# GpSimd operations that wait for the all-SBUF VectorE operation ahead of them in the plan

## The chip, the cores and the metric

The kernel runs on one core of a Trainium2 chip. The metric is device time in microseconds (us). The kernel before takes 2153.72 us, the median of 3 runs (2153.02 to 2155.7). A core has four engines that compute here: TensorE (PE, with its weight loads shown as PEld), VectorE (DVE), ScalarE (ACT) and GpSimd (POOL). SyncE (SP) issues the DMAs. Each engine works through its instructions in the order in which they stand in the program, and waits on semaphores where it needs what another engine makes. PE reads its operands from SBUF and adds into PSUM; DVE and ACT reach both; POOL works on SBUF alone.

## The reference

One decoder layer on x of 1 x 1024 x 1024 (sequence 1024, width 1024), in float32:

```python
h = rmsnorm(x, norm_mix)
proj = h @ w_in                       # z, xBC, dt, lru_y, lru_x, q, k, v, g, three gates
y_ssd, y_lru, y_ret = ssd_mixer(...), rglru_mixer(...), retention_mixer(...)
branch_d = jnp.einsum('bskw,kwd->bskd', branches, w_branch)
merged = jnp.sum(sigmoid(gate_pre) * branch_d, axis=2)
x = x + merged @ w_o
h = rmsnorm(x, norm_ffn)
a, u = jnp.split(h @ ffn_w_in, 2, axis=-1)          # 3072 columns each
a = causal_dwconv(a, ffn_conv_w, ffn_conv_b)        # 3 taps
x = x + (gelu(a) * u) @ ffn_w_out
return rmsnorm(x, norm_final)
```

Most of the work is dense products: the input projection, three branch products, `w_o`, and the two products of the FFN.

## The kernel before

**Products.** Activations lie transposed, 128 channels x 1024 positions, in two halves of 512 positions. Every dense product is made in "quads": a 2 x 2 block product (two output strips, two halves of positions) by a Strassen-Winograd scheme of seven products instead of eight. Each float32 operand is split into a high part (ACT copies it into the matmul's type, `h`) and a low part (the rest, `l`), and a product is three matmuls: high x high, high x low, low x high (L450, L451, L452). A quad sums in the PSUM banks x, y and z, and what leaves a bank is copied or added by ACT (L260) and DVE (L475, L480) into SBUF buffers named `e_...`.

**Sets and strips.** The activations of a stage are a set of seven operands B11, B21, T1, T2, T3, B22, T4, four tiles each, made by `build_set`: `sub` subtracts two SBUF tiles into PSUM (L342, and L353 for the second difference, tiles `hT`, `y2T`, `g0T` ...), and `split` makes `h` on ACT and `l` on DVE or POOL (L336, `g0B22l` and the like). The sets follow one another: h (the projection), y0, y2 and y1 (the branches), mg (`w_o`), h2 (FFN in), g0, g1 and g2 (FFN out, a third of the inner channels each). The weights of each quad come by DMA in strips (`wr_...`); `Quad.operand` makes their sums S1 to S4 (L407), S1 and S3 in PSUM banks of their own, and `Quad.prep` splits them (ACT, and L420 on DVE or POOL: `fo00A12l` is quad fo00's low part of A12). When a quad's result is complete, its `use` function runs: L1162 and L1166 gate and add the branches (`e_br`), L1230 multiplies the FFN's two halves (`cv_fa`), L1253 adds the residual (`e_fo`). The FFN's convolution (`conv`) pads a tile with three zeros (MEMSET, L522, `o_fa`), scales it on ACT and adds two taps on DVE (L528).

**What sets the order.** All operations are recorded first, with their buffers, the engines that may do them and a due time. `Plan.schedule` then plays the program through with an estimated duration for each, gives each operation an engine and a start, and the program is issued in the order of the starts, under `manual_schedule`, so that each engine's order is the plan's. The variable `port` of the planner keeps two kinds of operation from overlapping in the plan: any POOL operation, and a DVE operation with the mark `lock`, which is set where nothing that the operation reads lies in PSUM:

```python
o.lock = "DVE" in engs and len({id(b) for b in r if b.tag in PSUMS}) == 0
...
ok = not (port > t and (e == "POOL" or (e == "DVE" and o.lock))) and fits(o)
...
if e == "POOL" or (e == "DVE" and o.lock):
    port = t + dur
```

This holds in the plan, with its estimated durations. On the chip the engines run by their semaphores alone, and in the kernel before nothing orders a POOL operation against a DVE operation that shares no data with it.

Of the kernel before, what the change touches and what calls it, by code (L numbers as in the profile page):

```python
# [240 lines left out]
class K:  # L241
# [1103 lines left out]
    def run(self, gl):  # L1345
        tc, nc = self.tc, self.nc
        with tc.tile_pool(name="small", bufs=1) as small, \
                tc.tile_pool(name="big", bufs=1) as pool, \
                tc.tile_pool(name="psum", bufs=1, space=PSUM) as psum, \
                tc.tile_pool(name="dram", bufs=1, space=DRAM) as dpool:  # L1350
            self.small, self.dpool = small, dpool
            self.load_consts()
            self.record(gl)
            slots = dict(SLOTS)
            for key in self.OPS:
                for p in range(4):
                    for s in "hl":
                        slots[f"{key}{s}{p}"] = 1
            ops = self.pl.schedule(slots)
            eng = {"PE": nc.tensor, "ACT": nc.scalar, "DVE": nc.vector, "POOL": nc.gpsimd, "DMA": nc.sync}  # L1360
            with tc.manual_schedule():
                for op in ops:
                    for b in op.alloc:
                        pl = psum if b.tag in PSUMS else pool
                        b.t = pl.tile(b.shape, b.dt, name=b.name, tag=f"{b.tag}_{b.slot}")
                    op.fn(eng[op.eng])


def pairs():
# [97 lines left out]
```

## Time and profile before

| | |
|---|---|
| median of 3 runs | 2153.72 us |
| the profiled execution | 2152.18 us, of which 2150.3 are the span of its instructions |
| mean granted PE clock | 0.987 |
| ACT busy | 1265.2 us (59%) |
| HBM read and written | 236.34 MB, 94.37 MB |
| POOL's operations | 399 |

The profile is of one execution. Its page gives the busy time of each engine, and views of the trace give single instructions: the start in us from the start of the span, the duration, the engine, the line of the kernel, the operation, the tile written and the tiles read, and in square brackets how long the engine had been idle and which instruction released it. A row with "x3" stands for three such instructions in a row, with their time together. Stage windows cut the span in pieces and give each engine's busy time in each. A row that begins with an engine and has "<-" and another engine is a group of waits: the time in total, how many, and the longest.

### The profile page before, as it was taken

What the parts mean: (1) busy time and instruction counts of PE and PEld (TensorE: products, weight loads), DVE (VectorE), ACT (ScalarE), POOL (GpSimd) and SP (SyncE); (2) the same over time, 40 slices, a digit from 0 to 9 for tenths busy, and PEclk for the clock granted to TensorE, in tenths of its full rate; (3) what the DMA queues carried; (4) which work ended last, traced back from release to release, by engine and by line L of the source; (5) the groups of instructions that cost most, each with busy time, mean ns of one, the idle gap of its engine ahead of it and who ended that gap; (6) DMA issues with size and microseconds to landing.
All of it is one profiled execution on the core that took longest, in us unless ns stands there. A gap on an engine that the chain in (4) does not pass through costs nothing. (4 is left out here: it accounts for less than half of the span.)

```text
span 2150.3 us, 27983 instructions
## 1 busy us (share of the span) xinstructions
PE 2076.7 (97%) x9394; PEld 1661.1 (77%) x9394; DVE 1585.5 (74%) x2469; ACT 1265.2 (59%) x2182; POOL 490.6 (23%) x399
## 2 busy tenths in 40 slices
PE   8999999999999999999999999989999999999997
PEld 4788887778888887777777777768888888877775
DVE  7878889976544456665789889796676666787786
ACT  6656665455766689998744445465444444645453
POOL 3000023431011111111253332331111111233332
PEclk9999999999999999999999999989999999999999
DMA  5333335544344444446578755713322222366764
GB/s 179 118 106 125 108 122 168 167 141 139 130 145 155 150 156 152 150 157 207 188 236 280 245 181 191 240 57 105 103 103 80 78 89 79 108 226 224 227 212 159
DMA packets 148176, 332.56 MB, mean 155 GB/s; under 512 B 16448, under 2 KB 17216, under 8 KB 148032
## 3 DMA queue, kind: packets, MB, share of 16 engines
q1 hardware_dynamic: 148032, 330.78, 46.6%
q8 instruction: 73, 1.20, 0.2%
q14 instruction: 71, 0.58, 0.1%
HBM read 236.34 MB, written 94.37 MB: 154 GB/s over the span
## 5 line engine op out<-in xcount | busy, mean ns | idle before, releaser
L260 ACT ACT_TABLE_LOAD x94 | 120.6, 1283 | 1.8 <-DVE acc_fin L585 0.2
L260 ACT ACTIVATE cv_fa<-cv_fa 128x512 f32<-128x512 f32 x48 | 30.4, 632 | 56.4 <-DVE cv_fa L528 56.4
L528 DVE SCALAR_TENSOR_TENSOR cv_fa<-o_fa,consts,cv_fa 128x512 f32<-128x512 f32 x48 | 56.7, 1182 | 0.9
L1230 POOL TENSOR_TENSOR cv_fa<-cv_fa,o_fu 128x512 f32<-128x512 f32 x21 | 32.6, 1551 | 99.8 <-ACT o_fu L260 99.8
L528 DVE SCALAR_TENSOR_TENSOR cv_fa<-e_ff,consts,cv_fa 128x512 f32<-128x512 f32 x48 | 38.0, 792 | 4.9 <-ACT cv_fa L260 4.9
L260 ACT ACTIVATE mt<-ps_a,acs 128x128 f32<-128x128 f32 x128 | 38.9, 364 | 0.3
L1253 POOL TENSOR_TENSOR e_fo<-e_fo,xl 128x512 f32<-128x512 f32 x13 | 16.8, 1294 | 75.4 <-DVE e_fo L480 66.7
L260 ACT ACTIVATE e<-ps_a 64x512 f32<-64x512 f32 x32 | 19.0, 593 | 13.7 <-PE ps_a L855 13.2
L944 PE MATMUL ps_l<-lxh,lwh 128*128 128x512 f32 x64 | 26.0, 406 | 0.3
L1052 PE MATMUL ps_ry<-sc,vt 128*128 128x128 f32 x128 | 23.8, 278 | 2.2 <-DVE rst L1040 1.6
L1162 DVE TENSOR_TENSOR e_br<-e_br,gl 128x512 f32<-128x512 f32 x19 | 23.5, 1237 | 3.0 <-DMA gl<-gt 2.5
L867 DVE TENSOR_TENSOR mt<-mt,cbt 128x512 f32<-128x512 f32 x22 | 16.8, 763 | 11.8 <-ACT mt L260 11.7
L946 PE MATMUL ps_l<-lxh,lwl 128*128 128x512 f32 x64 | 25.2, 394 | 0.0
L945 PE MATMUL ps_l<-lxl,lwh 128*128 128x512 f32 x64 | 25.2, 394 | 0.0
L965 DVE TENSOR_TENSOR li<-li,lx 128x512 f32<-128x512 f32 x16 | 11.1, 693 | 18.4 <-ACT li L260 18.4
L1230 DVE TENSOR_TENSOR cv_fa<-cv_fa,e_ff 128x512 f32<-128x512 f32 x23 | 22.6, 984 | 2.3 <-ACT cv_fa L260 0.3
L1040 DVE SCALAR_TENSOR_TENSOR rst<-rst,ps_kv 128x128 f32<-128x128 f32 x40 | 11.0, 286 | 17.8 <-ACT rst L260 16.1
L475 DVE TENSOR_TENSOR e_ff<-e_ff,z_ff 128x512 f32<-128x512 f32 x24 | 16.5, 687 | 10.0 <-PE z_ff L452 10.0
L965 POOL TENSOR_TENSOR li<-li,lt 128x512 f32<-128x512 f32 x4 | 5.2, 1302 | 78.7 <-ACT lt L260 78.7
L867 POOL TENSOR_TENSOR mt<-mt,cbt 128x512 f32<-128x512 f32 x10 | 13.9, 1394 | 40.3 <-ACT mt L260 38.5
L965 DVE TENSOR_TENSOR li<-li,lt 128x512 f32<-128x512 f32 x12 | 8.3, 693 | 19.8 <-ACT lt L260 19.8
L528 DVE SCALAR_TENSOR_TENSOR cv_xs<-o_xs,consts,cv_xs 128x512 f32<-128x512 f32 x24 | 21.9, 912 | 0.5
(6169 smaller groups left out, 8082.1 us busy)
## 6 DMA issues: line engine op xcount, KB each, us to landing
wr_ff<-in_ffn_in_dram SPq DMA_DIRECT2D x50, 512.0 KB, 3.8
wr_fo<-in_ffn_out_dram SPq DMA_DIRECT2D x43, 512.0 KB, 4.6
wr_br<-in_w_branch_dram SPq DMA_DIRECT2D x36, 512.0 KB, 4.6
yl<-yd SPq DMA_DIRECT2D x60, 256.0 KB, 4.8
gl<-g SPq DMA_DIRECT2D x60, 256.0 KB, 4.5
wr_gt<-in_w_quads_dram SPq DMA_DIRECT2D x24, 512.0 KB, 5.0
gl<-gt SPq DMA_DIRECT2D x48, 256.0 KB, 4.0
g<-cv_fa SPq DMA_DIRECT2D x48, 256.0 KB, 2.1
```

Source lines behind the costliest of these rows:

```text
L260: e.activation(out(), in_(), func, **kw)
L475: k.vec(lambda e, e2=e2, ps=ps: e.tensor_tensor(e2.t[:, O:], e2.t[:, O:], ps.t, ALU.add), [e2, ps], [e2], prio=end)
L528: self.vec(lambda e, s=s: e.scalar_tensor_tensor(cv.t[:, O:], raw.t[:, O - s : W - s], w(taps - 1 - s), cv.t[:, O:], ALU.mult, ALU.add), [ ...
L867: self.vec(lambda e, mt=mt: e.tensor_tensor(mt.t[:, O:], mt.t[:, O:], cbt.t[:, O:], ALU.mult), [mt, cbt], [mt], pool=True)
L944: e.matmul(p_.t, wh.t[:, s], h.t, start=(k == 0), stop=False)
L945: e.matmul(p_.t, wh.t[:, s], l.t, start=False, stop=False)
L946: e.matmul(p_.t, wl.t[:, s], h.t, start=False, stop=(k == 1))
L965: mul = lambda a, b_: self.vec(lambda e: e.tensor_tensor(a.t[:, o], a.t[:, o], b_.t[:, o], ALU.mult), [a, b_], [a], pool=True)
L1052: e.matmul(py.t[:, d], at(x, s), at(sc, s), start=True, stop=first)
L1162: self.vec(lambda e: e.tensor_tensor(out.t[:, o], ap(), g.t[:, o], ALU.mult), [buf, g], [out], pool=not ps)
L1230: self.vec(lambda e: e.tensor_tensor(a.t[:, o], a.t[:, o], u.t[:, o], ALU.mult), [a, u], [a], pool=True)
L1253: self.vec(lambda e: e.tensor_tensor(out.t[:, o], ap(), x.t[:, o], ALU.add), [buf, x], [out], pool=not ps)
```

## The change

After each operation of the plan is issued, the kernel notes the last DVE operation that has `lock` (nothing that it reads lies in PSUM; where it writes does not matter) and whose function returns its instruction. Every POOL operation that follows in the plan gets a dependency on it. Nothing else is added.

```diff
@@ -1358,12 +1358,20 @@
             ops = self.pl.schedule(slots)
             eng = {"PE": nc.tensor, "ACT": nc.scalar, "DVE": nc.vector, "POOL": nc.gpsimd, "DMA": nc.sync}
+
+            info = mybir.DependencyInfo(mybir.DependencyClass.Sync, mybir.DependencyReason.DATA)
+            holder = None
             with tc.manual_schedule():
                 for op in ops:
                     for b in op.alloc:
                         pl = psum if b.tag in PSUMS else pool
                         b.t = pl.tile(b.shape, b.dt, name=b.name, tag=f"{b.tag}_{b.slot}")
-                    op.fn(eng[op.eng])
+                    ins = op.fn(eng[op.eng])
+                    if op.eng == "DVE" and op.lock and ins is not None:
+                        holder = ins
+                    elif op.eng == "POOL" and holder is not None:
+                        tc.add_manual_dep(ins.ins, holder.ins.name, info, reason="port order")
+
```

The sums of products in PSUM (S1 and S3, the differences of `sub`, the copies of banks) are already so in the kernel before; the diff does not touch them. The lines behind L1358 move by 8.

In the built program the order of every engine is what it was. The rows of PE and ACT are the same to the last wait. On POOL 145 of 404 rows have other waits, and the rows that wait for DVE go from 185 to 293; on DVE three rows have other waits; on SP 33 rows lose a wait for DVE. The places that the text below speaks of are these. The rows are those of the difference on POOL, with the waits at the end; a row that waits for DVE waits for one particular instruction of it, which the row does not name, and where two rows follow each other without a wait the second is held by the first.

POOL at the start of the branch product with set y2 (`y2B22l` are low parts of that set, made from the loaded tiles `yl`; `br22A11l` is a low part of a weight strip; L1162 gates a result):

```order
+L420 TENSOR_TENSOR br22A11l<-wr_br_10566,br22A11h 128x512 [waits DVE_49,DMAHW3_49,PE_49,Activation_49]
 L1162 TENSOR_TENSOR e_br_10611<-e_br_10611,gl_71_10598 128x512 [waits DVE_49]
 L336 TENSOR_TENSOR y2B22l_10739<-yl_41_10192,y2B22h_10718 128x512 [waits DMAHW6_49,Activation_49]
-L336 TENSOR_TENSOR y2B22l_10787<-yl_51_10246,y2B22h_10725 128x512 [waits Activation_49]
+L336 TENSOR_TENSOR y2B22l_10787<-yl_51_10246,y2B22h_10725 128x512 [waits DVE_49]
 L336 TENSOR_TENSOR y2B22l_10805<-yl_61_10268,y2B22h_10730 128x512 [waits DMAHW5_49,Activation_49]
```

`br22A11l` had no wait for DVE before; it now waits for the second of a pair of differences `y2T` (L342). The second `y2B22l` now waits for the split `br23A11l` (L420).

POOL at the passage from the FFN's first product to its second, where set g0 is made:

```order
-L336 TENSOR_TENSOR g0B11l_16886<-gl_20_13802,g0B11h_16859 128x512 [waits Activation_49]
+L336 TENSOR_TENSOR g0B11l_16886<-gl_20_13802,g0B11h_16859 128x512 [waits DVE_49]
 L336 TENSOR_TENSOR g0B11l_16905<-gl_30_13957,g0B11h_16877 128x512 [waits PE_49,Activation_49]
 L420 TENSOR_TENSOR fo01A12l<-wr_fo_16804,fo01A12h 128x512 [waits DVE_49,DMAHW2_49,PE_49,Activation_49]
-L336 TENSOR_TENSOR g0B22l_17029<-gl_41_14591,g0B22h_17007 128x512 [waits Activation_49]
+L336 TENSOR_TENSOR g0B22l_17029<-gl_41_14591,g0B22h_17007 128x512 [waits DVE_49,Activation_49]
 L420 TENSOR_TENSOR fo02A11l<-wr_fo_16889,fo02A11h 128x512 [waits DVE_49,DMAHW5_49,PE_49,Activation_49]
-L336 TENSOR_TENSOR g0T2l_17096<-gl_20_13802,g0T2h_17054 128x512 [waits Activation_49]
+L336 TENSOR_TENSOR g0T2l_17096<-gl_20_13802,g0T2h_17054 128x512 [waits DVE_49]
 L336 TENSOR_TENSOR g0B22l_17108<-gl_51_14603,g0B22h_17012 128x512
-L336 TENSOR_TENSOR g0B22l_17125<-gl_61_16973,g0B22h_17020 128x512 [waits DMAHW0_49]
+L336 TENSOR_TENSOR g0B22l_17125<-gl_61_16973,g0B22h_17020 128x512 [waits DMAHW0_49,DVE_49]
```

The first `g0B11l` now waits for the split `ff23A22l` (L420) of DVE, the first `g0B22l` for a `g0T` (L342), `g0T2l` for a product `cv_fa` (L1230), and behind `g0T2l` stand three `g0B22l` (the third follows the last row here), the second of them with a wait of its own for the next `g0T`. DVE's rows at that place are the same before and after:

```order
L336 TENSOR_TENSOR g0T1l_17045<-g0T_2_17022,g0T1h_17036 128x512
L528 SCALAR_TENSOR_TENSOR cv_fa_17049<-e_ff_16934,consts,cv_fa_17049 128x512
L407 TENSOR_TENSOR fo00S_2_17066<-wr_fo_17015 128x512
L528 SCALAR_TENSOR_TENSOR cv_fa_17049<-e_ff_16934,consts,cv_fa_17049 128x512
L1230 TENSOR_TENSOR cv_fa_16985<-cv_fa_16985,o_fu_17061 128x512
L420 TENSOR_TENSOR fo02A12l<-wr_fo_16889,fo02A12h 128x512
L1230 TENSOR_TENSOR cv_fa_17049<-cv_fa_17049,e_ff_16907 128x512
L420 TENSOR_TENSOR fo00S1l<-fo00S_2_17066,fo00S1h 128x512
L407 TENSOR_TENSOR fo00S_2_17066<-fo00S_2_17066,wr_fo_16943 128x512
```

The row for which `g0T2l` waits is the second L1230 here; fo00S and the `cv_fa` of L528 stand ahead of it.

POOL where set g1 is made:

```order
 L336 TENSOR_TENSOR g1T2l_17828<-gl_20_17273,g1T2h_17820 128x512 [waits DVE_49,Activation_49]
-L336 TENSOR_TENSOR g1B22l_17862<-gl_41_17365,g1B22h_17802 128x512 [waits PE_49]
+L336 TENSOR_TENSOR g1B22l_17862<-gl_41_17365,g1B22h_17802 128x512 [waits DVE_49,PE_49]
 L420 TENSOR_TENSOR fo12A12l<-wr_fo_17694,fo12A12h 128x512 [waits DMAHW6_49,PE_49,Activation_49]
-L336 TENSOR_TENSOR g1B22l_17927<-gl_61_17765,g1B22h_17822 128x512 [waits DMAHW1_49]
+L336 TENSOR_TENSOR g1B22l_17927<-gl_61_17765,g1B22h_17822 128x512 [waits DMAHW1_49,DVE_49]
 L336 TENSOR_TENSOR g1B22l_17945<-gl_71_17797,g1B22h_17836 128x512 [waits DMAHW5_49]
```

The first `g1B22l` now waits for a `g1T` (L342) besides PE, and the second in this piece for a later split of DVE.

At the start of the kernel the second `hB22l` waits for the second `hT`, and in set h2 the first `h2T2l` for the second of the `h2T` pair that stood beside it.

## The prediction

> **What bounds the kernel now.** I read the engines' shares first, then the span cut by stage, then who TensorE (PE) waits for.
>
> ```profile
> PE 2076.7 (97%) x9394; PEld 1661.1 (77%) x9394; DVE 1585.5 (74%) x2469; ACT 1265.2 (59%) x2182; POOL 490.6 (23%) x399
> ...
> 300.00:780.00 480.00, 471.20 (x2561) 386.71 (x2561) 324.80 (x563) 294.00 (x550) 107.48 (x81) 1.00 0.46 149
> 1000.00:1450.00 450.00, 418.99 (x1738) 332.00 (x1737) 371.09 (x536) 233.06 (x416) 154.22 (x112) 0.97 0.61 202
> 1450.00:1885.00 435.00, 434.95 (x1875) 351.42 (x1873) 295.87 (x438) 220.23 (x374) 69.99 (x70) 1.00 0.27 92
> 1885.00:2150.30 265.30, 241.26 (x1022) 193.30 (x1022) 206.11 (x294) 120.20 (x214) 82.20 (x59) 0.96 0.64 212
> ```
>
> A stage row gives start and end in us, the length, then busy time of PE, PEld, VectorE (DVE), ScalarE (ACT) and GpSimd (POOL), granted clock, DMA share and GB/s. PE is idle 73.6 us (2150.3 - 2076.7), and in bunches: 8.8 in 300 to 780, 31.0 in the branch products up to the FFN's start, 24.0 in the last stage. In 1450 to 1885 it is 0.05: nothing that DVE or POOL save there is worth anything. That stage also gives PE's pace, 435 / 1875 = 0.232 us a matmul.
>
> ```profile
> PE x_fo L450 <- ACT e_fo L260: 8.1, 3, 3.7
> PE x_wo L450 <- ACT e_wo L260: 4.0, 1, 4.0
> PE ss_fin L565 <- DVE acc_fin L585: 3.0, 1, 3.0
> PE y_gt L450 <- DVE e_gt L480: 2.4, 1, 2.4
> PE z_wo L450 <- DVE e_wo L480: 2.3, 1, 2.3
> ```
>
> These are some of PE's longest waits (total, times, longest). The largest names ACT, so the question is what ACT was late for. I follow it at 1888.63.
>
> ```profile
> 1888.63 0.79 PE L450 MATMUL x_fo<-g0B21h,fo00A12h 128*128 128x512 f32 x1 [3.68 <-ACT e_fo L260]
> ...
> 1893.91 0.61 PE L450 MATMUL x_fo<-g0B11h,fo01A11h 128*128 128x512 f32 x1
> ...
> 1886.97 0.63 ACT L260 ACTIVATE cv_fa<-cv_fa 128x512 f32<-128x512 f32 x1 [2.83 <-DVE cv_fa L528]
> ...
> 1863.94 2.39 DVE L336 TENSOR_TENSOR g0B11l<-gl,g0B11h 128x512 fp32r<-128x512 f32 x2
> 1866.26 1.78 DVE L420 TENSOR_TENSOR ff23A22l<-wr_ff,ff23A22h 128x512 fp32r<-128x512 f32 x1
> ...
> 1882.82 0.74 DVE L528 SCALAR_TENSOR_TENSOR cv_fa<-e_ff,consts,cv_fa 128x512 f32<-128x512 f32 x1
> 1883.48 1.79 DVE L407 TENSOR_TENSOR fo00S<-wr_fo 128x512 f32<-128x512 f32 x1
> 1885.19 1.75 DVE L528 SCALAR_TENSOR_TENSOR cv_fa<-e_ff,consts,cv_fa 128x512 f32<-128x512 f32 x1
> ...
> 1890.22 0.68 DVE L1230 TENSOR_TENSOR cv_fa<-cv_fa,e_ff 128x512 f32<-128x512 f32 x1
> ...
> 1883.22 1.50 POOL L336 TENSOR_TENSOR g0T2l<-gl,g0T2h 128x512 fp32r<-128x512 f32 x1 [0.93 <-ACT g0T2h L260]
> 1884.68 5.07 POOL L336 TENSOR_TENSOR g0B22l<-gl,g0B22h 128x512 fp32r<-128x512 f32 x3
> ```
>
> The same SCALAR_TENSOR_TENSOR takes 0.74 us at 1882.82 and 1.75 at 1885.19, where POOL has been at work since 1884.68; a clean TENSOR_TENSOR takes 0.68 (1890.22), one beside POOL 1.78. So an all-SBUF DVE operation that meets a running POOL operation pays 1.0 to 1.1 us, and POOL pays too (5.07 / 3 = 1.69). Through this ACT's cv_fa starts 2.83 late, the copy e_fo queued behind it on ACT is late, and PE stands 3.68. The stall has a second price: the twelve matmuls from 1888.63 to 1893.91 take 5.28 us instead of 12 x 0.232 = 2.8, so 2.5 more.
>
> [...]
>
> **The change part by part.** No instruction is added to or moved on any engine or on the DMA queue; POOL rows gain waits for DVE, and some rows of the DMA queue lose one, which releases nothing earlier, since POOL's wait stands ahead of it. The gain is what is no longer blocked, the cost what becomes late.
>
> *g0, 1888.63.* In the built program g0T2l waits for cv_fa<-cv_fa,e_ff (1890.22), and three g0B22l stand behind it on POOL. None of them is there when DVE runs fo00S and cv_fa: 1.1 + 1.0 = 2.1 earlier on ACT's chain. g0B11l of POOL is held in the same way until ff23A22l (1866.26), which frees that row and the second of the pair ahead of it (2.39 - 2 x 0.68), 1.1 + 1.0 = 2.1 more in a queue that runs without a break. Together that exceeds 3.68, so I take the whole stall and its slow matmuls: 3.7 + 2.5 = **6.2**. With the first two alone, 2.1 + 2.5 = 4.6.
>
> *g1, 1973.58.*
>
> ```profile
> 1966.97 1.78 DVE L420 TENSOR_TENSOR fo12A11l<-wr_fo,fo12A11h 128x512 fp32r<-128x512 f32 x1
> 1968.67 1.78 DVE L342 TENSOR_TENSOR g1T<-gl,gl 128x512 f32<-128x512 f32 x1
> ...
> 1966.45 1.75 POOL L336 TENSOR_TENSOR g1B22l<-gl,g1B22h 128x512 fp32r<-128x512 f32 x1
> ...
> 1970.49 0.60 ACT L260 ACTIVATE g1T1h<-g1T 128x512 fp32r<-128x512 f32 x1 [3.29 <-DVE g1T L342]
> ...
> 1973.58 0.79 PE L450 MATMUL x_fo<-g1B21h,fo10A12h 128*128 128x512 f32 x1 [3.52 <-ACT e_fo L260]
> ```
>
> g1B22l now waits for that g1T, so both DVE rows fall to 0.68: 2 x 1.1 = 2.2. The gap shrinks to 1.3, well under the 3.14 of y2, so the 2.5 of slow matmuls go as well: **4.7**.
>
> *y2, 1145.54.*
>
> ```profile
> 1133.68 2.39 DVE L342 TENSOR_TENSOR y2T<-yl,yl 128x512 f32<-128x512 f32 x2
> 1139.77 1.77 DVE L1162 TENSOR_TENSOR e_br<-e_br,gl 128x512 f32<-128x512 f32 x1
> 1141.47 2.38 DVE L342 TENSOR_TENSOR y2T<-yl,yl 128x512 f32<-128x512 f32 x2
> ...
> 1138.00 4.69 POOL L336 TENSOR_TENSOR y2B22l<-yl,y2B22h 128x512 fp32r<-128x512 f32 x3
> ...
> 1145.54 0.50 PE L450 MATMUL x_br<-y2B21h,br20A12h 128*128 128x512 f32 x1 [3.14 <-ACT e_br L260]
> ...
> 1147.18 0.63 PE L450 MATMUL x_br<-y2B21h,br20A12h 128*128 128x512 f32 x1
> ...
> 1150.17 0.44 PE L451 MATMUL x_br<-y2B11l,br22A11h 128*128 128x512 f32 x1
> ```
>
> Of the three y2B22l the second now waits for a split that ran behind these rows; e_br (1.77 - 0.68) and the blocked one of the later pair of y2T (2.38 - 2 x 0.68) are freed, 1.1 + 1.0 = 2.1. POOL's br22A11l, held until the second y2T of 1133.68, frees another 1.0 (2.39 - 2 x 0.68). With 3.1 that is the whole stall of 3.14. The seven matmuls from 1147.18 to 1150.17 take 2.99 instead of 1.62, so 1.4 more: **4.5**. Lower end 2.1.
>
> *The other waits.* For these I have samples only.
>
> ```profile
> 45.34 3.48 DVE L342 TENSOR_TENSOR hT<-x,x 128x512 f32<-128x512 f32 x2
> 1082.59 1.78 DVE L407 TENSOR_TENSOR br01S<-wr_br,wr_br 128x512 f32<-128x512 f32 x1
> 1416.93 3.15 DVE L342 TENSOR_TENSOR h2T<-e_wo,x 128x512 f32<-128x512 f32 x2
> 2139.41 1.45 PE L575 MATMUL ss_fin<-consts,acc_fin 128*128 128x128 f32 x8 [0.57 <-DVE acc_fin L574]
> ```
>
> Both hT and both h2T are freed; br01S is not, since the POOL operation beside it stands ahead of the wait; and a freed DVE operation is not always on PE's path. So of the idle time that can go I take half. In 1000 to 1450: 31.0 less what has no blocked pair ahead of it (x_wo 4.0, y_gt 2.4, z_wo 2.3) and less y2's 3.1 leaves 19.2, half is 9.6. In 300 to 780: half of 8.8, 4.4. At the start the two hT, 3.48 - 2 x 0.68 = 2.1. In the last stage 24.0 less g0 and g1 (7.2), ss_fin (3.0 and 0.6) and the 9.4 behind the last matmul (2139.41 + 1.45 to 2150.3) leaves 3.8, half is 1.9. Together **18.0**, with ends 0 and 34.
>
> *What the waits cost.*
>
> ```profile
> L522 POOL MEMSET o_fa<- 128x3 f32 x22 | 2.2, 102 | 2.8 <-DMA g<-cv_fa 2.8
> 1416.56 1.29 POOL L336 TENSOR_TENSOR h2T2l<-x,h2T2h 128x512 fp32r<-128x512 f32 x1 [0.81 <-ACT h2T2h L260]
> L451 PE MATMUL y_ff<-h2T2l,ff0S2h x4: 392/398/421, 1423.1 to 1425.2; 128*128 128x512 f32 x4
> ```
>
> The 22 pads (MEMSET) of the FFN now wait for DVE too, and ACT's first step of each convolution waits for the pad: 0.1 for the pad and as much for two hand-overs (g1T ends at 1970.45, ACT starts at 1970.49), 0.2 each, 4.4 in all. The convolutions are hidden by the products of 1450 to 1885, where PE idles 0.05, so I cost them 0; without that cover 4.4.
>
> Splits that move later: the closest is h2T2l. The first is now held until the second h2T ends, at 1420.1 by the trace of before, two splits of 1.3 then end at 1422.7, and the first reader is at 1423.1: in time by 0.4. I put in two places where one clean POOL operation is late, 2 x 1.3 = **2.6**; ends 0 and 5.2.
>
> Sum: 6.2 + 4.7 + 4.5 + 18.0 - 2.6 = 30.8 less. The profiled execution took 2152.2 us (2150.3 of span), so the changed kernel would take 2121.4 there; the median of the three runs shown is 1.5 higher, and from it the forecast is 2153.7 - 30.8 = **2123**.
>
> **The rivals.** *The block only changes its owner.* A POOL operation released by one DVE operation starts into the next, and blocks that. For it: DVE runs back to back at these places, so the next is at hand. Against it: in g0 and y2 the blockers stand in rows of three or four, and one wait holds the row past the stretch that ACT needs. Price: all gains go, 2152 to 2156. Chance 0.09.
>
> [...]
>
> *Late splits: the side that ends slower.* POOL works in strict order, so one held operation holds all behind it. If the splits of a set end after their first matmul is due, which for h2T2l begins 0.4 us beyond what I worked out, PE stands at each of the eight set changes. At one POOL operation each (1.3) and a hand-over (0.1), with the gains gone, that is 8 x 1.4 = 11 more: 2165. Chance 0.07.
>
> *More than half.* If every wait that I didn't set aside goes and no split is late, the gain is 6.2 + 4.7 + 4.5 + 34 = 49: 2104. Chance of that or less 0.05.
>
> **How the numbers follow.** The forecast case has 0.79. Its low end is that 49, 2105. Its high end takes the three places at their lower values, nothing from the other waits and both ends of late splits: 4.6 + 4.7 + 2.1 - 5.2 = 6.2 less, 2147. A difference under 0.2% (4.3 us) can't be told from no change: faster 0.84 (the first and the last case), same 0.09, slower 0.07.
>
> **What would show it.** Right: no x_fo gap above 2 us at the first products of g0 and g1 and no 0.63 us matmuls behind them; fo00S near 0.68 and the cv_fa behind it near 0.74; PE idle 40 to 50 us instead of 73.6; POOL's splits at 1.3 each instead of up to 1.75; DVE's busy time down by tens of us. Wrong: PE waits that name POOL at the first products of a set, as many DVE rows of 1.78 as before at other places, or PE idle in 1450 to 1885 behind pads.

## The result and the profile after

The changed kernel takes 2121.27 us (median of 4 runs, 2119.98 to 2122.05) against 2153.37 us of the kernel before (median of 4 runs, 2147.83 to 2155.7): 32.1 us less, a ratio of 0.985 with a 95% interval of 0.983 to 0.987. The forecast was 2123.

First the engines' shares, the two stages from the FFN's middle on, cut in the same places of the program as before (1450 and 1885 there), and PE's longest waits, all of the kernel after.

```profile
PE 2065.1 (97%) x9394; PEld 1651.8 (78%) x9394; DVE 1564.5 (74%) x2469; ACT 1264.2 (60%) x2182; POOL 459.6 (22%) x399
...
1430.00:1864.60 434.60, 434.53 (x1874) 351.30 (x1872) 298.45 (x440) 220.63 (x375) 62.90 (x68) 1.00 0.27 93
1864.60:2120.00 255.40, 236.54 (x1022) 189.77 (x1022) 200.51 (x292) 119.84 (x214) 78.49 (x60) 0.98 0.66 221
...
PE x_wo L450 <- ACT e_wo L260: 4.0, 1, 4.0
PE x_br L450 <- ACT e_br L260: 3.7, 8, 0.9
PE x_fo L450 <- ACT e_fo L260: 3.6, 3, 1.6
PE ss_fin L565 <- DVE acc_fin L585: 3.0, 1, 3.0
```

The last stage, with the same 1022 matmuls, takes 255.4 us instead of 265.3, and PE idles 18.9 in it instead of 24.0; the FFN's middle is as it was. The waits of x_fo fall from 8.1 to 3.6 us, the longest from 3.7 to 1.6; x_wo and ss_fin, which were set aside, are as they were. PE's idle time is 2120.0 - 2065.1 = 54.9 instead of 73.6, so 18.7 of the span's 30.3 us are idle time. The other 11.6 are in PE's busy time, where slow matmuls count as busy: the twelve of before from 1888.63 to 1893.91 fill all 5.28 us there, at a granted clock of 0.50. The mean granted clock rises from 0.987 to 0.992, and the 128x512 matmuls that start 0.43 us behind the one ahead of them, instead of the usual 0.23, fall from 95 to 52. These 43, at nearly 0.2 each, make 8.4 of the 11.6; they are of the kind that the stalls of g0, g1 and y2 had behind them. POOL's busy time fell by 31.0 us, since 7 of its operations are blocked where 86 were; DVE's fell by 21.0.

Here "blocked" means that an instruction takes over 0.25 us more than the quickest of its line, operation and shape. By that count 173 DVE instructions were blocked before (135.5 us in all) and 153 after (114.0). The order on DVE is the same, so they can be compared one by one: 120 are blocked in both, 53 were freed, 33 are new.

Next g0 after the change, as it was shown of before: DVE, POOL and PE.

```profile
1860.31 0.69 DVE L353 TENSOR_TENSOR gl<-gl,g0T 128x512 f32<-128x512 f32 x1 [1.68 <-ACT g0T1h L260]
1860.91 0.16 DVE L524 COPY e_ff<-halo 128x3 f32<-128x3 f32 x1
...
1861.58 1.56 DVE L528 SCALAR_TENSOR_TENSOR cv_fa<-e_ff,consts,cv_fa 128x512 f32<-128x512 f32 x1
1863.07 0.68 DVE L407 TENSOR_TENSOR fo00S<-wr_fo 128x512 f32<-128x512 f32 x1
1863.67 0.74 DVE L528 SCALAR_TENSOR_TENSOR cv_fa<-e_ff,consts,cv_fa 128x512 f32<-128x512 f32 x1
...
1861.31 1.29 POOL L420 TENSOR_TENSOR fo02A11l<-wr_fo,fo02A11h 128x512 fp32r<-128x512 f32 x1 [1.83 <-DVE e_ff L524]
1866.29 1.29 POOL L336 TENSOR_TENSOR g0T2l<-gl,g0T2h 128x512 fp32r<-128x512 f32 x1 [3.70 <-DVE cv_fa L1230]
...
1866.10 0.50 PE L450 MATMUL x_fo<-g0B21h,fo00A12h 128*128 128x512 f32 x1 [1.56 <-ACT e_fo L260]
```

g0T2l waits for the cv_fa of L1230 as built, fo00S takes 0.68 and the second tap 0.74, and the matmuls behind the stall are at full speed. A stall of 1.56 is left: another POOL operation, fo02A11l, was released by the small COPY at 1860.91 and met the first tap, which took 1.56. Then g1 and y2:

```profile
1941.92 0.68 DVE L420 TENSOR_TENSOR fo12A11l<-wr_fo,fo12A11h 128x512 fp32r<-128x512 f32 x1
1942.53 0.68 DVE L342 TENSOR_TENSOR g1T<-gl,gl 128x512 f32<-128x512 f32 x1
...
1943.35 1.30 POOL L336 TENSOR_TENSOR g1B22l<-gl,g1B22h 128x512 fp32r<-128x512 f32 x1 [1.91 <-DVE g1T L342]
...
1946.34 0.50 PE L450 MATMUL x_fo<-g1B21h,fo10A12h 128*128 128x512 f32 x1 [1.35 <-ACT e_fo L260]
...
1128.18 1.85 DVE L420 TENSOR_TENSOR br22A12l<-wr_br,br22A12h 128x512 fp32r<-128x512 f32 x1 [0.36 <-ACT br22A12h L260]
1129.95 0.68 DVE L1162 TENSOR_TENSOR e_br<-e_br,gl 128x512 f32<-128x512 f32 x1
1130.55 1.29 DVE L342 TENSOR_TENSOR y2T<-yl,yl 128x512 f32<-128x512 f32 x2
...
1128.19 1.29 POOL L336 TENSOR_TENSOR y2B22l<-yl,y2B22h 128x512 fp32r<-128x512 f32 x1
1132.52 2.52 POOL L336 TENSOR_TENSOR y2B22l<-yl,y2B22h 128x512 fp32r<-128x512 f32 x2 [3.04 <-DVE br23A11l L420]
...
1133.53 0.50 PE L450 MATMUL x_br<-y2B21h,br20A12h 128*128 128x512 f32 x1 [0.69 <-ACT e_br L260]
1143.37 0.50 PE L450 MATMUL x_br<-y2B21h,br22A12h 128*128 128x512 f32 x1 [0.81 <-ACT e_br L260]
```

At g1 both DVE rows are clean and the gap is 1.35. At y2 the freed rows are clean, 0.69 of the 3.14 is left, and a new gap of 0.81 stands ahead of the third quad. At 1128.18 DVE starts 0.01 us ahead of POOL, whose operation follows straight on its last one, and DVE pays all the same: at such a tie the starts don't tell who wins.

### The profile page after: what moved, and what is told of

It is laid out like the page before. It is cut to its first block, busy times and chain, and to the rows that moved or that the text cites. A ratio compares the mean times of both kernels' runs of the same rounds, so it can differ in the third digit from the quotient of the medians.

```text
span 2120.0 us, 28043 instructions
## 1 busy us (share of the span) xinstructions
PE 2065.1 (97%) x9394; PEld 1651.8 (78%) x9394; DVE 1564.5 (74%) x2469; ACT 1264.2 (60%) x2182; POOL 459.6 (22%) x399
## 5 line engine op out<-in xcount | busy, mean ns | idle before, releaser
L528 DVE SCALAR_TENSOR_TENSOR cv_fa<-o_fa,consts,cv_fa 128x512 f32<-128x512 f32 x48 | 57.1, 1189 | 0.9
L1230 POOL TENSOR_TENSOR cv_fa<-cv_fa,o_fu 128x512 f32<-128x512 f32 x21 | 27.2, 1295 | 112.8 <-ACT o_fu L260 59.2
L528 DVE SCALAR_TENSOR_TENSOR cv_fa<-e_ff,consts,cv_fa 128x512 f32<-128x512 f32 x48 | 36.8, 766 | 4.7 <-ACT cv_fa L260 4.6
L1230 DVE TENSOR_TENSOR cv_fa<-cv_fa,e_ff 128x512 f32<-128x512 f32 x23 | 28.3, 1230 | 2.3 <-ACT cv_fa L260 0.3
L528 DVE SCALAR_TENSOR_TENSOR cv_xs<-o_xs,consts,cv_xs 128x512 f32<-128x512 f32 x24 | 21.9, 912 | 0.5
L1162 DVE TENSOR_TENSOR e_br<-e_br,gl 128x512 f32<-128x512 f32 x19 | 19.6, 1034 | 3.2 <-DMA gl<-gt 2.6
```

The costliest lines, as they stand in the source:

```text
L528: self.vec(lambda e, s=s: e.scalar_tensor_tensor(cv.t[:, O:], raw.t[:, O - s : W - s], w(taps - 1 - s), cv.t[:, O:], ALU.mult, ALU.add), [ ...
L1162: self.vec(lambda e: e.tensor_tensor(out.t[:, o], ap(), g.t[:, o], ALU.mult), [buf, g], [out], pool=not ps)
L1230: self.vec(lambda e: e.tensor_tensor(a.t[:, o], a.t[:, o], u.t[:, o], ALU.mult), [a, u], [a], pool=True)
```

## The experiments

**One place earlier.** The theory: where an all-SBUF DVE operation and a POOL operation meet, who comes first decides which of them pays, and at some places on PE's path DVE must come first. How exactly must the wait name the pair? ("The port" in the expectations is the planner's `port`, which keeps the two kinds apart in the plan; the runs show how long the operations of such pairs take, not by what means one holds up the other.)

```diff
-                        holder = ins
-                    elif op.eng == "POOL" and holder is not None:
-                        tc.add_manual_dep(ins.ins, holder.ins.name, info, reason="port order")
+                        older, holder = holder, ins
+                    elif op.eng == "POOL" and older is not None:
+                        tc.add_manual_dep(ins.ins, older.ins.name, info, reason="port order")
```

> Every POOL operation waits for the locked DVE operation one place ahead of the one of the change, so it is released while that last one still has to run. Theory (who comes first at the port decides, and DVE must come first): it depends on the hand-over. In the kernel before, DVE starts its next operation some 0.06 us ahead of the printed end of the last, while POOL starts 0.08 us after a release; so DVE still wins wherever its queue runs without a break, and most of the gain stays, about 25 us (2128). Rival A (the waits must name the right pair, POOL released one operation early takes the port): half or less of the gain, 2138 or more. Rival B (later POOL operations help by themselves, by buffers or DMA): the delays are some 0.7 us shorter each, gain a little smaller, 2122 to 2130; this run does not tell B from the theory, the next one does.

Measured: 2120.47 us, 32.9 less than before, ratio 0.984 (0.982 to 0.986). Rival A falls. The rows of DVE and POOL at g0 in this kernel show why:

```profile
1868.85 0.68 DVE L420 TENSOR_TENSOR fo02A12l<-wr_fo,fo02A12h 128x512 fp32r<-128x512 f32 x1
1869.45 0.68 DVE L1230 TENSOR_TENSOR cv_fa<-cv_fa,e_ff 128x512 f32<-128x512 f32 x1
...
1869.61 1.66 POOL L336 TENSOR_TENSOR g0T2l<-gl,g0T2h 128x512 fp32r<-128x512 f32 x1 [3.82 <-DVE fo02A12l L420]
```

The release comes when fo02A12l ends (1869.53); DVE has its next operation under way at 1869.45, POOL starts at 1869.61, and it is POOL that pays (1.66). Of POOL's operations 90 are blocked here, where the kernel before has 86 and the changed one 7, and the time is the changed kernel's: what POOL pays costs nothing that can be measured.

**Two places earlier.** As above, with the third last locked operation in place of the second last (`holders[-3]` of a list).

> The same number of waits, each for the locked DVE operation two places ahead of the one of the change. Theory: POOL is now released while one locked DVE operation runs and another still stands behind it, so it gets the port between them; the blocks at g0, g1 and y2 come back, and 20 or more of the 30 us with them: 2140 to 2152. Rival B (any delay or thinning of POOL helps): the delay per operation shrinks from the change's by two operations of 0.7 us only, most of the gain stays, 2122 to 2132.

Measured: 2141.64 us, 11.7 less than before, ratio 0.994 (0.993 to 0.996). Two thirds of the gain go, so it is not delay as such that helps, and rival B falls. The block is back where the wait no longer stands behind what PE needs, as at g1 in this kernel:

```profile
1961.54 0.68 DVE L420 TENSOR_TENSOR fo12A11l<-wr_fo,fo12A11h 128x512 fp32r<-128x512 f32 x1
1962.14 1.78 DVE L342 TENSOR_TENSOR g1T<-gl,gl 128x512 f32<-128x512 f32 x1
...
1961.76 1.61 POOL L336 TENSOR_TENSOR g1B22l<-gl,g1B22h 128x512 fp32r<-128x512 f32 x1 [0.69 <-DVE e_fo L1253]
...
1967.06 0.50 PE L450 MATMUL x_fo<-g1B21h,fo10A12h 128*128 128x512 f32 x1 [2.45 <-ACT e_fo L260]
```

g1B22l starts 0.22 behind fo12A11l and is still at work when g1T starts at 1962.14, and g1T pays 1.1 (1.78 instead of 0.68): the gap is 1.35 + 1.1 = 2.45. At g0 I was wrong: two places back is still behind the second tap, and the gap there was 0.72.

**The waits turned round.**

```diff
-                        holder = ins
-                    elif op.eng == "POOL" and holder is not None:
-                        tc.add_manual_dep(ins.ins, holder.ins.name, info, reason="port order")
+                        if pooled is not None:
+                            tc.add_manual_dep(ins.ins, pooled.ins.name, info, reason="port order")
+                    elif op.eng == "POOL":
+                        pooled = ins
```

> The waits are turned round: a locked DVE operation waits for the POOL operation that precedes it in the plan, and POOL waits for nothing of the kind. The two kinds are then just as little on the port together as in the change. Theory (POOL has time, DVE has not): DVE pays the whole POOL operation as a wait instead of as a block, and pays it also where it used to come first; no gain, 2153 to 2175. Rival C (the loss lies in the overlap itself, both pay about 1 us for each met pair): taking the overlap away in either direction gains, 2120 to 2135.

Measured: 2167.61 us, 14.3 more than before, ratio 1.006 (1.004 to 1.008). Only 55 DVE instructions are blocked, and DVE's busy time is the lowest of all kernels here, yet it is the slowest:

```profile
PE 2078.6 (96%) x9394; PEld 1660.4 (77%) x9394; DVE 1512.3 (70%) x2469; ACT 1262.4 (58%) x2182; POOL 485.0 (22%) x399
...
PE x_fo L450 <- ACT e_fo L260: 9.3, 3, 4.7
PE x_br L450 <- ACT e_br L260: 8.5, 6, 3.4
```

DVE's waits that name POOL grow from 2.6 us in 4 waits to 118.5 in 149, more than the 80 us by which its blocks shrink (135.5 to 55.8): the block became a longer wait, and the waits of x_fo and x_br grow too (8.1 and 7.3 before). Rival C falls: the overlap as such is not the loss, DVE's place in it is.

**Only the sets, and all but the sets.** The first adds to the condition that the POOL operation writes a low part of a set, the second that it does not.

```diff
-                    elif op.eng == "POOL" and holder is not None:
+                    elif op.eng == "POOL" and holder is not None and (op.alloc[0].tag or "" if op.alloc else "")[:-2] in self.OPS:
```

> Only POOL's low parts of the sets (L336) get the wait; the weights' low parts, the gates, FFN products, residuals and pads do not. Theory: the blockers of g0, g1, y2, h2 and hT are all L336, so their gains stay (6.2 + 4.7 + 4.5 and the start's 2.1 of the forecast, and what the other sets add), 18 to 25 us: 2128 to 2135. Rival D (the gain is spread evenly over all POOL operations): L336 is about 130 of the 363 long POOL operations, so a third of 32, 2142.

Measured: 2128.07 us, 25.3 less, ratio 0.989 (0.987 to 0.990). The number of L336 operations in that expectation was wrong: the trace has 81 among POOL's 399, so rival D would have given 6.5 us (2147), which is farther off still.

> The complement of the run with sets only: every POOL operation but the low parts of the sets (L336) waits. Theory: what is left of the whole, 32 less 25, so 4 to 9 us: 2144 to 2150, with the stalls of g1 and y2 there as in the kernel before. Rival (either half alone is enough, since POOL's order passes a wait on to what stands behind): 15 us or more, under 2138.

Measured: 2150.02 us, 3.7 less, ratio 0.998 (0.997 to 0.999), just short of the 4 to 9 that were expected. The gap is 2.75 at y2, near the 3.14 of before, and 4.46 at g0, where it was 3.68; at g1 it is 2.43 and not the 3.52 that was expected, since g1T is clean there (0.69) and only fo12A11l is blocked (1.78). The halves do not reach the whole (25.3 + 3.7 = 29.0 of 32), but within the intervals they add.

**By place.** From g0 on alone, and up to the FFN alone (each by a flag that a name in the plan's order sets).

> The change for POOL operations from the first g0B11l on, none ahead of it. Theory: the gains of g0 and g1 and of the last stage alone: 4.7 + 5.0 by the profile of after, 10.9 and 1.9 by the forecast: 9 to 13 us, 2141 to 2145; all stalls ahead of 1880 us as before. Rival (what is gained late is only passed on from earlier stages): no gain or under 4, 2150 or more.

Measured: 2143.3 us, 10.4 less, ratio 0.995 (0.993 to 0.997).

> The change for POOL operations up to the start of the FFN (ahead of the weight strip ff3, at about 1446 us of the profile of after), none behind it. With the run from g0 on it leaves out only the middle of the FFN. Theory (savings where PE does not stand are worth nothing, and the gains of separate places add): 32 less the 10 of the run from g0 on, 20 to 23 us, 2131 to 2134; the stalls of g0 and g1 as in the kernel before. Rival (the FFN's own waits gain or cost): if the two parts sum to 27 or less the middle gains the rest; if to 36 or more it costs.

Measured: 2129.73 us, 23.4 less, ratio 0.990 (0.987 to 0.992). The two parts sum to 33.8 against the whole of 32.1: within the intervals they add, and the middle of the FFN is worth nothing that can be measured. The stalls of g0 and g1 stand there as before (3.59 and 3.52).

**Pads.** `op.engs["POOL"] > 0.3` in the condition leaves the pads without the added wait.

> The change without the waits on the pads (MEMSET, L522) of POOL. Theory: the convolutions are hidden behind the products, so nothing changes, 2118 to 2125. Rival (the pads' waits cost the 4.4 us worked out without cover, or more): 2113 to 2117.

Measured: 2119.79 us, ratio 0.984 (0.983 to 0.986) against 0.985 (0.983 to 0.987) of the change. The pads' waits cost nothing that can be measured.

**What is left at g0.** The condition leaves out the one operation fo02A11l.

> The change, but POOL's fo02A11l (L420), which stands ahead of g0T2l, has no added wait. In the profile of after it was released by a 3-column COPY of DVE, started at 1861.31 and blocked the first tap of cv_fa (1.56 us instead of 0.74), and a stall of 1.56 us was left at the first product of g0. Theory (that block is what is left over of the stall, by the release of a POOL operation in front of a locked DVE operation): it starts about 1.5 us earlier, beside operations that read PSUM, the tap takes 0.74 and the stall falls to 0.7 or 0.8, as in the run with the wait one place earlier. Rival (something else sets the stall, such as ACT's queue): 1.5 us as before. The time, 1 us less at most, can't tell.

Measured, in a single run: POOL, DVE and PE of this kernel at that place.

```profile
1858.14 1.29 POOL L420 TENSOR_TENSOR fo02A11l<-wr_fo,fo02A11h 128x512 fp32r<-128x512 f32 x1 [0.33 <-ACT fo02A11h L260]
...
1859.98 0.73 DVE L528 SCALAR_TENSOR_TENSOR cv_fa<-e_ff,consts,cv_fa 128x512 f32<-128x512 f32 x1
...
1863.67 0.50 PE L450 MATMUL x_fo<-g0B21h,fo00A12h 128*128 128x512 f32 x1 [0.75 <-ACT e_fo L260]
```

The tap is clean and the gap 0.75 instead of 1.56. The one time, 2118.72, can't tell 0.8 us. But the block is only half of what was left, as two other kernels with the same waits at this place show. In the run without pads, and in the run from g0 on, the tap is blocked too (1.57 in both), and the gap is 0.50 and 1.02. Here are the tap and the gap without pads:

```profile
1858.17 1.57 DVE L528 SCALAR_TENSOR_TENSOR cv_fa<-e_ff,consts,cv_fa 128x512 f32<-128x512 f32 x1
1862.69 0.50 PE L450 MATMUL x_fo<-g0B21h,fo00A12h 128*128 128x512 f32 x1 [0.50 <-ACT e_fo L260]
```

And this is what ACT waited for a little earlier in the profile after:

```profile
1858.06 0.63 ACT L260 ACTIVATE g0B22h<-gl 128x512 fp32r<-128x512 f32 x1 [1.15 <-DMA gl<-g]
```

That row of ACT stands ahead of g0T1h, for which DVE waits. It had waited 1.15 us for the DMA of a tile `gl` in the profile after, 1.08 in this run, 0.06 without pads, and 0.58, for PE, in the run from g0 on. The gap less this wait is 0.41 to 0.44 in the three kernels with the block and -0.33 both here and in the run with the wait one place earlier. So the block is worth 0.75, and the rest of the stall comes and goes with ACT's wait: the theory and its rival are each right for about half.

**The kernel before once more.**

> The kernel before, unchanged, for a second profile of it. It tells which of the differences between the two profiles belong to the change and which to the execution. Theory: the stalls at g0, g1, y2 and of the hT pair are there again within 0.5 us, since order and blocks make them; the 2.4 us in front of y_gt, which shrank to 1.0 with the change though no blocked pair stands ahead of it, and the long half-speed stretch behind the first x_ff vary by execution. Rival: those two are there again as well, and then the change did something to them that I have not named. Time 2153, ratio 1.

Measured: 2151.94 us, ratio 1.000 (0.999 to 1.001). In this second profile the stalls at g0, g1 and y2 are 3.53, 3.55 and 2.85, and the hT pair takes 3.49. The first x_ff is followed by matmuls at full speed (0.39 to 0.40 each at 1400.31 to 1401.00, where the first profile has 0.63 at 1397.83 to 1399.11), so the half-speed stretch there was a difference of the execution and no part of the gain. The gap at y_gt is 1.41 where the first profile had 2.39, so it varies by execution too. But in the four profiles with the whole change ahead of it (after, up to the FFN, without pads, and the one of fo02A11l) it is 0.96 to 1.03, and never under 1.41 in the three without (before twice, and from g0 on). This second profile also shows a blocked pair there, on DVE and POOL ahead of y_gt:

```profile
1005.44 0.95 DVE L1156 TENSOR_TENSOR gl<-gl,acc_ssd 128x512 f32<-128x512 f32 x1 [2.65 <-DMA gl<-gt]
...
1004.55 1.29 POOL L420 TENSOR_TENSOR gt22A12l<-wr_gt,gt22A12h 128x512 fp32r<-128x512 f32 x1 [12.34 <-ACT gt22A12h L260]
```

The L1156 takes 0.69 in the profile after, where gt22A12l starts behind it (1001.37 against 1000.42). The rest of the gap goes with the DMA for which DVE waits. So a part of y_gt may belong to the change; how much stays open.

With two profiles of each kernel (before twice; the change, and the change without pads, which measures the same) the gain can be put in its place. The times run from the start of the first matmul of one stage to that of the next:

| stretch | before, again | after, without pads | mean gain | forecast |
|---|---|---|---|---|
| first z quad to first branch product | 1025.7, 1022.6 | 1017.5, 1017.1 | 6.9 | 6.5 |
| branch products | 249.3, 253.3 | 241.9, 243.6 | 8.6 | 14.1, with the row below |
| `w_o` to the FFN's fifth quad | 191.0, 189.7 | 184.4, 182.3 | 7.0 | in the row above |
| rest of the FFN's first product | 389.9, 389.9 | 389.7, 389.7 | 0.2 | 0 |
| g0's first quad to the last matmul | 260.2, 261.3 | 250.3, 250.5 | 10.4 | 12.8 |

(The forecast's parts: 4.4 and the start's 2.1; y2's 4.5 and 9.6; g0 6.2, g1 4.7 and 1.9.) The sum is 33.1.

## Why the prediction was right, point by point

**Bounds.** Right: the gain lies in the stretches where PE was idle, and the FFN's middle gives 0.2.

**g0.** The mechanism was right, the size was not: 6.2 forecast, and by the two profiles 3.68 - 1.56 = 2.1 of gap and 2.5 of slow matmuls, 4.6, the value given as the lower end. The step that failed is the 2.1 "in a queue that runs without a break", taken for g0B11l at 1864. DVE's queue does have breaks between there and the stall: 0.74 us ahead of 1881.48 in the trace of before, and 1.68 ahead of 1860.31 in the profile after, where it waits for ACT's g0T1h and so for the DMA ahead of it. What was freed early was waited out there. Of the 1.56 that was left over, 0.75 are the block of fo02A11l and the rest goes with ACT's wait for that DMA. The gap less ACT's wait is 1.95 or 1.96 in the three profiles without the change at this place (before twice, and up to the FFN) and some 0.42 with it, so 1.54 less, or 2.3 without the new block of the first tap: the 2.1 of fo00S and cv_fa came.

**g1.** Right: gap 1.3 forecast and 1.35 measured, no slow matmuls.

**y2.** 4.5 forecast; 3.14 - 0.69 of gap and 1.4 of slow matmuls, less the new gap of 0.81, make 3.0. The step that failed is that the whole stall goes: the first y2B22l is not held, and br22A12l pays more beside it than before (1.85 at 1128.18). The new gap seems to have another origin. The rows are br22A12l in the trace of before, and one of DVE ahead of the new gap in the profile after:

```profile
1138.82 1.03 DVE L420 TENSOR_TENSOR br22A12l<-wr_br,br22A12h 128x512 fp32r<-128x512 f32 x1 [0.36 <-ACT br22A12h L260]
...
1136.21 0.70 DVE L407 TENSOR_TENSOR br20S<-wr_br 128x512 f32<-128x512 f32 x1 [0.62 <-DMA wr_br<-in_w_branch_dram]
```

From the second row to the matmul at 1143.37 DVE has no break and no row over 0.70. In all seven kernels with the new gap (0.79 to 0.81) this row waits for the DMA of its strip and starts 7.16 us ahead of the matmul; in the five without the gap it doesn't wait. So the traces point to the strip's DMA and not to a block; no run changed that DMA.

**The other waits.** 18.0 forecast, as half of what could go; 6.9 + (15.6 less the 3.0 of y2) + (10.4 less 4.6 and 4.7) = 20.6 by the table. A half was a guess that held; it wasn't derived, and which blocks make up the 20.6 was not traced one by one. To leave out x_wo and z_wo was right (4.0 and 2.2 after). Whether it was right to leave out y_gt stays open: it is 0.4 to 1.4 shorter in the profiles with the change, and a part of that is the execution's.

**Late splits.** 2.6 forecast, none found. One wait of PE names POOL at the first products of a set, h2B11l ahead of x_ff, and it stood there before. The closest case was worked out from the trace of before, with both h2T blocked, though the same step had counted them as freed: after the change the two h2T2l run from 1399.74 to 1402.27 and the first reader is at 1404.4, so 2.1 us are to spare and not 0.4.

```profile
1399.74 2.53 POOL L336 TENSOR_TENSOR h2T2l<-x,h2T2h 128x512 fp32r<-128x512 f32 x2 [1.31 <-ACT h2T1h L260]
L451 PE MATMUL y_ff<-h2T2l,ff0S2h x4: 390/393/395, 1404.4 to 1406.5; 128*128 128x512 f32 x4
```

So the close agreement of 30.8 with 32.1 is partly luck: 3.1 too much at g0 and y2 stand against 2.6 of late splits and 2.6 in the other waits that were taken too low.

**The rivals.** "The block only changes its owner" is half true: 120 of the 173 blocked DVE instructions are blocked as before, and 33 are new ones. It decides little, because those that PE waited for at g0, g1 and y2 are among the 53 that were freed; fo02A11l, and br22A12l at y2, are the places found where a block that is new or longer cost PE something. The direction of the wait decides much: the same pairs cost 32 us less with the waits on POOL and 14 more with the waits on DVE. In the rows of before fo00S, begun at 1883.48 beside g0T2l, took 1.79 and ended 0.55 us behind it. A released POOL operation does meet another of DVE at times, as the 33 new blocks show, but it was rarely one that PE waits for. The slower rival did not happen.

**What would show it.** The x_fo gaps are under 2 us without slow matmuls behind them, fo00S and the cv_fa behind it are clean, and POOL's operations are clean but for 7. The sign against, as many blocked DVE rows elsewhere, came in part: the DVE rows of 1.6 to 2.2 us fall from 92 to 56, but 153 are still blocked by the count above, and DVE's busy time is down by only 21. PE's idle time was forecast at 40 to 50 and is 54.9: I had reckoned the slow matmuls at 6.4, but PE's busy time fell by 11.6, so more of the gain came by the clock (0.987 to 0.992) and less by idle time than I had forecast.

## What to carry to other kernels

Where operations of two engines block each other, as those of DVE and POOL do here (1.0 to 1.1 us for DVE at a pair), put the order so that the one with time to spare comes second, and let it wait; one place too early gave the same here (2120.47 us against 2121.27), and two places too early lost two thirds of the gain (2141.64). Don't judge such a change by DVE's busy time or by the number of its blocked instructions: the reversed waits had the least of both (1512.3 us, 55) and the longest time (2167.61 us). A saving counts where an engine on the path is late, and only as far as that lateness goes before the queue's next break (at g0 the row freed at 1864 was waited out in a break of 1.68).

## What the runs showed that I had not expected

The half-speed stretch behind a stall varies by execution at the same stall. At g0 twelve matmuls ran slow behind a gap of 3.68 in the first profile, none behind 3.59 in the run up to the FFN, where those behind the gap of 3.52 at g1 did:

```profile
1867.94 0.50 PE L450 MATMUL x_fo<-g0B21h,fo00A12h 128*128 128x512 f32 x1 [3.59 <-ACT e_fo L260]
1868.28 0.39 PE L451 MATMUL x_fo<-g0B21l,fo00A12h 128*128 128x512 f32 x1
...
1951.12 0.50 PE L450 MATMUL x_fo<-g1B21h,fo10A12h 128*128 128x512 f32 x1 [3.52 <-ACT e_fo L260]
...
1951.78 0.63 PE L452 MATMUL x_fo<-g1B21h,fo10A12l 128*128 128x512 f32 x1
```

Nor does the length of the gap tell: behind only 2.45, in the run with the waits two places earlier, and behind 2.43, in the run of all but the sets, both at g1, stand matmuls of 0.63 instead of 0.39. A forecast should carry such a term as a chance, not as a sum.

A POOL operation that is released by the end of a DVE operation starts some 0.08 us behind that end (the median of 96 such pairs of 128x512 in the profile after; 31 of them take 0.14 or more), and DVE starts its next one 0.08 us ahead of it. That is why a wait one place too early still lets DVE come first.
